# A decoder trunk on one core: work ordered by tasks in hand-written code, or by a list scheduler over a recorded graph

## The chip, the cores and the metric

The kernel runs on one core of a Trainium2 chip. The core's engines work side by side, each through its own list of instructions in the order in which the list was written: TensorE (PE) multiplies matrices, VectorE (DVE) and ScalarE (ACT) do elementwise work, GpSimd (POOL) helps them, and SyncE (SP) issues transfers between HBM and the on-chip memory. The metric is the device time of one launch in microseconds (us), lower is better.

## The reference

Two layers of a hybrid decoder; 256 prompt tokens and 8 sample tokens (264 columns in all) share the weights. In outline:

```python
def token_mixers(u, lp, ...):
    proj = u @ lp['w_in']                       # 2048 -> 5504 with padding
    (q, k, v, z, xbc, dt, mq, mk, mv, mo, mi, mf) = split(proj)
    att = swa_prompt(q, k, v, sinks) / swa_sample(...)      # window 128, cached keys for the samples
    y   = ssd_scan(causal_conv(xbc), dt, A, B, C, S0)       # Mamba-2, chunks of 128
    y   = rms_norm((y + d_skip * xs) * silu(z), ssm_norm)   # two groups of 512
    h   = rms_norm(mlstm_scan(mq, mk, mv, mi, mf, C0, n0, m0)) * sigmoid(mo)
    return concatenate([att, y, h]) @ lp['w_out'], new_states
def decoder_layer(x, lp, ...):
    x = x + token_mixers(rms_norm(x, norm_mix), lp, ...)
    u = rms_norm(x, norm_mlp)
    return x + square(relu(u @ lp['w_up'])) @ lp['w_down']
```

A final RMSNorm follows. The new key, value, convolution, SSM and mLSTM states are outputs too.

## The kernel before

Weights stream from HBM once. The unit is a **half**: a block of 8 x 128 x 128 weights, 512 KB, 748 of them. SP loads it (`raw`), ACT casts it to a rounded form (`hi`, L163), DVE subtracts to get the remainder (`lo`, L164), and PE multiplies it in 24 matmuls of 264 columns: 16 with `hi` against the two parts of the activations (L1249, L1250), 8 with `lo` (L1252). `raw`, `hi` and `lo` have three buffers each, so the splits can be at most three halves ahead. Two halves make a **group** of 128 output columns of `w_in`.

In each layer the halves come in this order: `w_in` 86 halves (groups: gates, k, v, q, convolution B/C, convolution x, then 12 groups m of the mLSTM, 8 groups z that gate the SSD's output, 4 groups o), `w_out` 32 halves (the first 16 need the mix tiles `hA`/`lA`, the other 16 `hB`/`lB`), then the MLP's 256. The halves of layer 0 are numbered 0 to 373, those of layer 1 from 374.

The mixers' own small work (attention, SSD scan, mLSTM, norms) is woven between the halves. It is written as Python generators, "tasks", in the list `active`. Before each half the main loop lets the tasks go on until their stated costs pass `BUDGET = 1.7`, with flags (`setf`, `wait`) that keep a step back by one or more halves:

```python
        run_evacs()
        load(i + 4)
        cut(i + 2)
        run_later()
        run_tasks()
```

So the order on every engine is that of the source's own steps. Small PSUM results take four `ms` and two `sg` buffers, sums of halves two `acc`. The norm of the SSD's output, `y_norm`, is run once for each of two groups of 512: a matmul with ones spreads the sum of squares (`ms<-ysq`, L198), eight DVE steps take the inverse root (`rsqrt`, L168 to L175), then `xs` is scaled (L1042), cast and split into `hA`/`lA` or `hB`/`lB`.

Of the kernel before, what the change touches and what calls it, by code (L numbers as in the profile page):

```python
# [17 lines left out]
L = 2  # L18
P = 128
# [21 lines left out]
def trunk(ctx, tc, I, O):  # L41
    nc = tc.nc
    vec, act, pool, pe = nc.vector, nc.scalar, nc.gpsimd, nc.tensor
# [38 lines left out]
    slot = [0]  # L82
    flags = {}
    active = []
    evacs = []
    later_ = []

    def setf(name):
        flags[name] = slot[0]

    def ok(name, lag=1):
        return name in flags and slot[0] >= flags[name] + lag

    def wait(*names, lag=1):
        while not all(ok(n, lag) for n in names):
            yield 0.0

    def later(fn, n=1):
        later_.append((slot[0] + n, fn))

    def run_later(force=False):
        due = [x for x in later_ if force or x[0] <= slot[0]]
        for x in due:
            later_.remove(x)
            x[1]()

    def run_tasks():
        spent = 0.0
        for g in list(active):
            try:  # L110
                spent += next(g)
            except StopIteration:
                active.remove(g)
            if spent > BUDGET:
                break

    def run_evacs():
        while evacs:
            fn, need = evacs[0]
            if not all(ok(n) for n in need):  # L120
                return
            evacs.pop(0)
            fn()

    def tick():
# [7 lines left out]
    xt = cp.tile([P, KB, T], F32, name="xt")  # L133
    cst = cp.tile([P, C_SEL], F32, name="cst")
    cst2 = tb([P, C_N - C_SEL])
    vecs = [cp.tile([P, V_N], F32, name=f"vec{l}") for l in range(L)]
    wfin = cp.tile([P, KB], F32, name="wfin")
# [3 lines left out]
    ones = cp.tile([P, P], F32, name="ones")  # L141
    zeros = cp.tile([64, P], F32, name="zeros")
    sgn = cp.tile([P, 1], F32, name="sgn")
    pool.memset(ones, 1.0)
    warm = st((P, 1), "coef")
    A(out=warm, in_=ones[:, 0:1], func=AF.Exp)
    pool.memset(zeros, 0.0)
    pool.memset(sgn, 1.0)
    pool.memset(sgn[32:64], -1.0)
    identb = cp.tile([P, P], BF16, name="identb")  # L150
    maskb = cp.tile([P, 2, P], BF16, name="maskb")
    sel = cp.tile([P, 64], F32R, name="sel")
    ssel = cp.tile([P, 24], F32R, name="ssel")

    uh = cp.tile([P, KB, T], F32R, name="uh")
    ul = cp.tile([P, KB, T], F32R, name="ul")
    ssq = cp.tile([P, T], F32, name="ssq")
    rb = cp.tile([P, T], F32, name="rb")
    UU = [(uh[:, k], ul[:, k]) for k in range(KB)]

# [5 lines left out]
    def rsqrt(y, v, t):  # L166
        """y = v ** -0.5: a first guess from the bits, then a step of third order and one of second order."""
# [1218 lines left out]
```

## Time and profile before

| | |
|---|---|
| three runs | 2396.3, 2398.72, 2400.55 us; median 2398.72 |
| profiled execution, its span (first to last instruction) | 2391.9 us |
| profiled execution, around its span | not given apart; 2398.72 - 2391.9 = 6.8 us if it ran at the median |
| PE busy | 2327.1 us, 97% of the span |
| DVE busy | 1509.1 us, 63% |
| ACT busy | 1097.3 us, 46% |
| POOL busy | 435.9 us, 18% |
| mean granted TensorE clock | 0.993 |

The span covers the work between the first and the last instruction. Busy time is a sum over the whole span and says nothing of a single stretch: the mixers of layer 0 lie at about 40 to 452 us, its MLP up to 1199 us, the mixers of layer 1 at 1199 to 1629 us, its MLP up to 2376 us, and the final norm behind.

### The profile page before, as it was taken

Reading aid. Unit: us, or ns where it says so; the run is one execution under the profiler, and the core shown is the slowest. Engines: PE = TensorE matmul, PEld = TensorE weight load, DVE = VectorE, ACT = ScalarE, POOL = GpSimd, SP = SyncE. Lnnn points to the kernel's source line nnn. Section 1 sums busy time; section 2 is a strip of 40 time slices with the busy share of each in tenths; the row PEclk is TensorE's granted clock in tenths of the full one; section 3 lists DMA queues with packets and bytes.
Section 4 is the critical chain, followed back from the end, with each engine's and each line's share of the span. In section 5 each row is a group of like instructions: output and inputs, shape, how many; then the busy total and the mean of one; then the engine's idle time right before and its main releaser. Section 6 shows DMA issues by size and latency. Waiting matters only on the chain.

```text
span 2391.9 us, 45993 instructions
## 1 busy us (share of the span) xinstructions
PE 2327.1 (97%) x18874; PEld 2305.8 (96%) x18874; DVE 1509.1 (63%) x2179; ACT 1097.3 (46%) x1700; POOL 435.9 (18%) x408
## 2 busy tenths in 40 slices
PE   7999989999999999999999999999999999999997
PEld 7898989999999999999999989899999999999997
DVE  8778996754555454455686799866545545544544
ACT  5545544543353354354445454445434434534542
POOL 4226541400000000001441274332000000000023
PEclk9999999999999999999999999999999999999998
DMA  7456766555555555555554566555555555555553
GB/s 238 141 165 197 197 202 187 177 183 180 183 179 184 178 184 178 184 181 181 179 177 136 177 213 187 177 179 182 180 183 179 182 181 184 178 183 179 184 178 132
DMA packets 123474, 432.26 MB, mean 181 GB/s; under 512 B 15744, under 2 KB 18432, under 8 KB 123264
## 3 DMA queue, kind: packets, MB, share of 16 engines
q1 hardware_dynamic: 122688, 428.10, 56.9%
q8 instruction: 149, 2.44, 0.4%
q10 hardware_dynamic: 576, 1.22, 0.1%
q14 instruction: 61, 0.50, 0.1%
HBM read 410.10 MB, written 19.16 MB: 179 GB/s over the span
## 4 chain that ended last, share of the span: by engine, by line
PE 88%; DVE 9%; issue 1%; ACT 1%; POOL 1%; DMA 0%; DVEq 0%; ACTq 0%; POOLq 0%
PE acc L1250 28%; PE acc L1252 28%; PE acc L1249 28%; DVE lo L164 3%; DVE eB L669 1%; PE ms L685 0%; DMA raw<-in_w_in 0%; PE ms L468 0%; PE sg L447 0%; DVE ra L1027 0%; DVE tb L971 0%; PE ms L460 0%; DVE xt L1262 0%; ACT uh L179 0%; DVE ul L182 0%
## 5 line engine op out<-in xcount | busy, mean ns | idle before, releaser
L163 ACT CAST hi<-raw 128x1024 fp32r<-128x1024 f32 x748 | 786.3, 1051 | 1046.5 <-PE acc L1250 969.6
L164 DVE TENSOR_TENSOR lo<-raw,hi 128x1024 fp32r<-128x1024 f32 x745 | 931.7, 1251 | 347.0 <-ACT hi L163 346.4
L1249 PE MATMUL acc<-uh,hi 128*128 128x264 f32 x3392 | 859.1, 288 | 6.8 <-ACT uh L179 6.8
L1250 PE MATMUL acc<-ul,hi 128*128 128x264 f32 x3392 | 854.0, 287 | 4.3 <-DVE ul L182 4.3
L1249 PEld LDWEIGHTS acc<-uh,hi 128*128 128x128 f32 x3392 | 643.7, 190 | 10.1 <-ACT uh L179 6.8
L1250 PEld LDWEIGHTS acc<-ul,hi 128*128 128x128 f32 x3392 | 645.3, 190 | 8.2 <-DVE ul L182 5.0
L1252 PE MATMUL acc<-uh,lo 128*128 128x264 f32 x3392 | 481.0, 283 | 3.4 <-DVE lo L164 3.4
L1252 PEld LDWEIGHTS acc<-uh,lo 128*128 128x128 f32 x3392 | 442.9, 189 | 3.8 <-DVE lo L164 3.8
L1249 PE MATMUL acc<-hA,hi 128*128 128x264 f32 x1280 | 316.2, 283 | 0.0
L1249 PE MATMUL acc<-hB,hi 128*128 128x264 f32 x1280 | 316.2, 283 | 0.0
L1250 PE MATMUL acc<-lB,hi 128*128 128x264 f32 x1280 | 315.4, 283 | 0.0
L1250 PE MATMUL acc<-lA,hi 128*128 128x264 f32 x1280 | 315.4, 283 | 0.0
L187 POOL TENSOR_TENSOR ssq<-xt 128x264 f32<-128x264 f32 x4 | 6.1, 1522 | 1431.4 <-DVE xt L1143 1313.7
L1249 PEld LDWEIGHTS acc<-hB,hi 128*128 128x128 f32 x1280 | 241.3, 189 | 0.0
L1249 PEld LDWEIGHTS acc<-hA,hi 128*128 128x128 f32 x1280 | 241.3, 189 | 0.0
L1250 PEld LDWEIGHTS acc<-lB,hi 128*128 128x128 f32 x1280 | 240.3, 188 | 0.0
L1250 PEld LDWEIGHTS acc<-lA,hi 128*128 128x128 f32 x1280 | 240.3, 188 | 0.0
L1143 DVE TENSOR_TENSOR xt<-acc,xt 128x264 f32<-128x264 f32 x128 | 55.3, 432 | 205.0 <-PE acc L1252 205.0
L1252 PE MATMUL acc<-hB,lo 128*128 128x264 f32 x1280 | 183.2, 285 | 0.0
L1252 PE MATMUL acc<-hA,lo 128*128 128x264 f32 x1280 | 183.2, 285 | 0.0
L1135 DVE SCALAR_TENSOR_TENSOR ra<-acc,rb 128x264 f32<-128x264 f32 x128 | 55.3, 432 | 196.8 <-PE acc L1252 196.7
L1252 PEld LDWEIGHTS acc<-hB,lo 128*128 128x128 f32 x1280 | 167.0, 188 | 0.0
(394 smaller groups left out, 1861.0 us busy)
## 6 DMA issues: line engine op xcount, KB each, us to landing
raw<-in_w_up SPq DMA_DIRECT2D x256, 512.0 KB, 3.6
raw<-in_w_down SPq DMA_DIRECT2D x256, 512.0 KB, 3.6
raw<-in_w_in SPq DMA_DIRECT2D x172, 512.0 KB, 3.7
raw<-in_w_out SPq DMA_DIRECT2D x64, 512.0 KB, 3.6
S<-in_ssm SPq DMA_DIRECT2D x16, 512.0 KB, 4.6
out_ssm_s<-S SPq DMA_DIRECT2D x16, 512.0 KB, 2.8
S<-in_mC SPq DMA_DIRECT2D x8, 512.0 KB, 4.6
out_C_s<-S SPq DMA_DIRECT2D x8, 512.0 KB, 3.1
```

The costliest lines, as they stand in the source:

```text
L163: act.copy(out=hi, in_=src)
L164: (f or tt)(out=lo, in0=src, in1=hi.bitcast(F32), op=SUB)
L187: f(out=total, in0=src, in1=src, op=MUL)
L669: tt(out=wT[:, i], in0=E[:, i], in1=cbg, op=MUL)
L1135: stt(out=r, in0=acc, scalar=0.0, in1=rb, op0=MAX, op1=MUL)
L1143: tt(out=xt[:, g], in0=acc, in1=xt[:, g], op=ADD)
L1249: pe.matmul(acc, lhsT=h[:, k], rhs=rh, start=it.first and k == 0, stop=False)
L1250: pe.matmul(acc, lhsT=h[:, k], rhs=rl, start=False, stop=False)
L1252: pe.matmul(acc, lhsT=o[:, k], rhs=it.rhs(k)[0], start=False, stop=it.last and k == 7)
```

## The change

The code that computes is kept, but instructions are no longer issued when the source reaches them. `Program.record` writes each down as a node of a graph, with the regions of tiles that it reads and writes; `price` gives it a cost from a formula; `issue` first works backwards through the graph for a time by which each node is due, and then forwards through a model of five engines: it picks, again and again, the instruction that can start first. `emit` hands a free buffer to each tile at that moment (three `raw`/`hi`/`lo`, four `ms`, two `sg`, two `acc`, as before). Tasks, flags, `wait`, `BUDGET` and `tick` go away. The diff, cut to its core:

```diff
-BUDGET = 1.7
...
-    for i, it in enumerate(items):
-        slot[0] += 1
...
-        run_evacs()
-        load(i + 4)
-        cut(i + 2)
-        run_later()
-        run_tasks()
...
+class Program:
+    LAG = 0.06
+    AHEAD = 6.0
+    EARLY = 30.0
+    LOOSE = ("ms", "sg", "ra", "ac", "eA", "eB")
...
+        def room(n):
...
+                if not empty or (q[h] is not s and (len(empty) < 2 or s.tag not in self.LOOSE)):
+                    return None
...
+                for n in seen:
+                    a = room(n)
+                    if a is None:
+                        continue
+                    r = max(n.ready, a)
+                    s = max(t, r)
+                    k = (max(s - t, 0.08), self.rank(e, n))
+                    if pick is None or k < pick[0]:
+                        pick = (k, s, n)
...
+            if n.port:
+                n.cost += 0.6 * min(n.cost, max(0.0, port["POOL" if e == "DVE" else "DVE"] - s))
...
+    def rank(self, e, n):
+        if e == "PE":
+            return (n.weight, n.i)
+        return (min(n.kind, 1), n.due)
...
+        for ks in (range(0, 4), range(4, 8)):
+            with pr.bundle(True):
...
+        if l == 0:
+            accs = [acc_tile(), acc_tile(), ms_tile([P, T]), ms_tile([P, T])]
+            for g, acc in enumerate(accs):
+                half(acc, I["w_in"][l, g][:, 0:8], u_rhs(0), True, False)
```

Two things follow from these lines. On PE `rank` puts any small matmul that is ready ahead of a bundle of weight matmuls. And `room` gives a buffer of a tag to the tile that is next in the program's order, or, for the tags in `LOOSE`, to another one only while two buffers are empty. The last lines let the first four groups of layer 0 do their first halves before their second ones, with four accumulators. The splits of the attention's part of the mix move into `y_norm`. The counts of instructions are the same on each engine; what changes is their order and which buffer each uses. Every instruction of the kernel after carries the line of `emit`, L398.

PE, layer 0, the first `y_norm`. Before, its spreading matmul stands between the halves 71 and 72 (`acc_3443` and `acc_3583` are sums of `w_in`):

```order
L1252 MATMUL acc_3443<-uh_86,lo_3362 128x264 x8
L198 MATMUL ms_3551<-ysq_3186,ones_73 128x264
L970 MATMUL ms_3575<-srow_3237,ssel_85 128x512
L970 MATMUL ms_3579<-srow_3237,ssel_85 128x512
L1249 MATMUL acc_3583<-uh_86,hi_3413 128x264
```

In the changed kernel it stands behind the last half of `w_in` (85) and just ahead of half 86, the first of `w_out`, which needs its result in `hA_2619` and `lA_2703` (`acc_4176` is the sum of half 86, `acc_4212` that of half 87):

```order
L398 MATMUL ms_4133<-ysq_3305,ones_69 128x264
L398 MATMUL sg_4451<-srow_3578,ssel_220 128x512
L398 MATMUL sg_4804<-srow_3578,ssel_220 128x512
L398 MATMUL sg_4503<-srow_3578,ssel_220 128x512
L398 MATMUL acc_4176<-hA_2619,hi_3977 128x264
L398 MATMUL acc_4212<-hA_2619,hi_4023 128x264
L398 MATMUL ms_4170<-ysq_4148,ones_69 128x264
L398 MATMUL acc_4176<-lA_2703,hi_3977 128x264
L398 MATMUL acc_4176<-hA_2619,hi_3977 128x264
L398 MATMUL acc_4212<-lA_2703,hi_4023 128x264
L398 MATMUL acc_4176<-lA_2703,hi_3977 128x264
L398 MATMUL acc_4176<-hA_2619,hi_3977 128x264
```

The norm moved 14 halves later, and no half of `w_in` is left between it and the one that reads its result.

DVE, the same norm. Before, its steps are spread out between the splits of four halves (`lo<-raw,hi`):

```order
L164 TENSOR_TENSOR lo<-raw,hi 128x1024
L202 TENSOR_SCALAR ysq<-ms 128x264
L971 TENSOR_TENSOR tb<-ms,S_3439 128x512 x2
L1027 SCALAR_TENSOR_TENSOR ra<-ac,ra 128x264
L168 TENSOR_SCALAR Bb<-ysq 128x264
L1028 TENSOR_TENSOR xs<-xs,ra 128x264
L164 TENSOR_TENSOR lo<-raw,hi 128x1024
L169 SCALAR_TENSOR_TENSOR ac<-Bb 128x264
L975 TENSOR_REDUCE cqs<-tb 128x4
L170 TENSOR_TENSOR ac<-ac,ysq 128x264
L171 SCALAR_TENSOR_TENSOR ac<-ac 128x264
```

In the changed kernel the steps follow on rows of the mLSTM's sample work (`mw`, `sb`, `cqs`, `ns`, `tb<-sg,S`); the first row is the split of half 88:

```order
L398 TENSOR_TENSOR lo<-raw,hi 128x1024
L398 COPY mw<-ms 128x2
L398 SCALAR_TENSOR_TENSOR lB<-lB,EG,ms 128x129 x4
L398 TENSOR_TENSOR tb<-sg,S_4050 128x512
L398 COPY mw<-ms 128x2
L398 COPY sb<-ms 128x64
L398 SCALAR_TENSOR_TENSOR mw<-mw 128x4
L398 TENSOR_REDUCE cqs<-tb 128x4
L398 TENSOR_TENSOR ns<-m_1826,sb 128x32
L398 TENSOR_SCALAR ysq<-ms 128x264
L398 TENSOR_TENSOR mw<-mw,q2c 128x4
L398 SCALAR_TENSOR_TENSOR ms_4173<-sb 128x32
```

Behind these come 35 more rows without a split; the next `lo`, of half 89, is the 47th row behind that of half 88. What was spread over several halves now stands in one block.

SP, the very start. Before, one block of weights goes first, then `vecs` and most of the input `xt<-in_x`:

```order
L1182 DMA raw<-in_w_in 128x1024
L1196 DMA vec_70<-in_vecs 128x131
L1193 DMA xt<-in_x 128x528 x2
L1193 DMA xt<-in_x 128x1056 x2
L1182 DMA raw<-in_w_in 128x1024
L1193 DMA xt<-in_x 128x1056
L1182 DMA raw<-in_w_in 128x1024
L1204 DMA tb<-in_cst 128x344
```

Now three blocks of weights go ahead of all of `x`:

```order
L398 DMA raw<-in_w_in 128x1024 x3
L398 DMA vec_80<-in_vecs 128x131
L398 DMA xt<-in_x 128x528 x2
L398 DMA xt<-in_x 128x1056 x3
L398 DMA cst<-in_cst 128x656
L398 DMA scv<-in_scv 128x384
L398 DMA tb<-in_cst 128x344
L398 DMA S_105<-in_kt 128x1032
L398 DMA S_107<-in_vc 128x1024
```

The first `x` thus stands behind two more blocks of 512 KB in the queue.

## Rows read from the trace of the kernel before

**Rows 1.** The page: busy time, chain that ended last, the splits' group.

```profile
PE 2327.1 (97%) x18874; PEld 2305.8 (96%) x18874; DVE 1509.1 (63%) x2179; ACT 1097.3 (46%) x1700; POOL 435.9 (18%) x408
...
PE 88%; DVE 9%; issue 1%; ACT 1%; POOL 1%; DMA 0%; DVEq 0%; ACTq 0%; POOLq 0%
...
L164 DVE TENSOR_TENSOR lo<-raw,hi 128x1024 fp32r<-128x1024 f32 x745 | 931.7, 1251 | 347.0 <-ACT hi L163 346.4
```

**Rows 2.** Windows: the span by stages; busy us of each engine, its instructions in brackets.

```profile
core 0: us, PE busy (x) PEld busy (x) DVE busy (x) ACT busy (x) POOL busy (x), PEclk, DMA share, GB/s
0.00:40.00 40.00, 27.23 (x188) 25.77 (x189) 30.19 (x45) 23.24 (x37) 17.42 (x26) 1.00 0.72 248
40.00:166.00 126.00, 120.47 (x979) 118.29 (x978) 99.79 (x211) 64.86 (x124) 36.26 (x71) 1.00 0.50 158
166.00:196.00 30.00, 29.24 (x214) 26.38 (x213) 20.34 (x24) 12.16 (x23) 9.11 (x5) 1.00 0.58 178
196.00:270.00 74.00, 68.89 (x544) 67.17 (x544) 69.52 (x90) 38.05 (x114) 55.38 (x23) 0.98 0.64 215
270.00:359.00 89.00, 80.11 (x612) 77.60 (x611) 80.47 (x159) 43.03 (x112) 35.99 (x30) 0.96 0.69 192
359.00:452.00 93.00, 93.00 (x768) 93.00 (x768) 67.58 (x101) 45.62 (x57) 33.71 (x29) 1.00 0.60 184
452.00:1199.00 747.00, 746.88 (x6151) 746.61 (x6150) 395.52 (x475) 331.45 (x401) 36.11 (x32) 1.00 0.58 181
...
1250.00:1343.00 93.00, 91.69 (x747) 90.14 (x747) 68.57 (x142) 50.84 (x101) 19.18 (x46) 1.00 0.48 151
1343.00:1373.00 30.00, 29.30 (x215) 26.44 (x213) 20.26 (x23) 12.31 (x24) 9.12 (x5) 1.00 0.56 174
1373.00:1447.00 74.00, 68.78 (x540) 67.07 (x541) 69.25 (x90) 37.25 (x114) 55.29 (x23) 0.98 0.65 215
1447.00:1536.00 89.00, 80.44 (x614) 77.93 (x613) 80.65 (x159) 43.94 (x113) 34.57 (x26) 0.96 0.59 177
...
2376.00:2392.00 16.00, 0.72 (x3) 0.30 (x2) 10.62 (x23) 0.51 (x1) 3.59 (x4) 0.60 0.35 135
```

**Rows 3.** Waits of PE: matmul and releaser: us in total, times, longest.

```profile
PE ms L685 <- DVE eB L669: 11.8, 10, 1.8
PE ms L981 <- DVE tb L971: 10.1, 4, 3.2
...
PE acc L1252 <- DVE lo L164: 3.4, 2, 2.7
```

**Rows 4.** Timeline of DVE in layer 0's SSD: start us, us, instruction.

```profile
225.05 3.08 DVE L164 TENSOR_TENSOR lo<-raw,hi 128x1024 fp32r<-128x1024 f32 x1
...
230.22 1.21 DVE L164 TENSOR_TENSOR lo<-raw,hi 128x1024 fp32r<-128x1024 f32 x1
...
238.69 0.94 DVE L669 TENSOR_TENSOR eB<-eA,lA 128x256 f32<-128x256 f32 x2 [1.14 <-ACT eA L665]
```

**Rows 5.** Timeline of POOL, same stretch.

```profile
224.66 2.39 POOL L777 TENSOR_TENSOR S<-S,tb 128x1024 f32<-128x1024 f32 x1
```

**Rows 6.** DVE groups by shape, 0 to 470 us: busy us, mean ns.

```profile
L164 DVE TENSOR_TENSOR lo<-raw,hi 128x1024 fp32r<-128x1024 f32 x123 | 161.3, 1312 | 17.3 <-ACT hi L163 17.1
...
L669 DVE TENSOR_TENSOR eB<-eA,lA 128x256 f32<-128x256 f32 x16 | 18.4, 1169 | 2.4 <-ACT eA L665 2.1
```

**Rows 7.** Timeline of DVE in the second `y_norm` of layer 0.

```profile
353.41 0.43 DVE L202 TENSOR_SCALAR ysq<-ms 128x264 f32<-128x264 f32 x1
353.75 0.18 DVE L1001 SCALAR_TENSOR_TENSOR ms<-ms,ms 128x32 f32<-128x32 f32 x1
...
354.20 0.43 DVE L169 SCALAR_TENSOR_TENSOR ac<-Bb 128x264 f32<-128x264 f32 x1
```

**Rows 8.** Timeline of PE, two of its first matmuls.

```profile
9.56 0.42 PE L1250 MATMUL acc<-ul,hi 128*128 128x264 f32 x1
9.78 0.42 PE L1249 MATMUL acc<-uh,hi 128*128 128x264 f32 x1
```

More of the change, by code (lines that the diff above doesn't have):

```diff
@@ L79, in tb @@
         return st(shape, "tb", bufs=2)
[L82 to L125, printed above, removed]
-        slot[0] += 1
-        run_evacs()
-        run_later()
-        run_tasks()
[L133 to L137, printed above, removed]
+    xt = st((P, KB, T), "xt")
+    cst = st((P, C_SEL), "cst")
+    cst2 = tb((P, C_N - C_SEL))
+    vecs = [st((P, V_N), f"vec{l}") for l in range(L)]
+    wfin = st((P, KB), "wfin")
     ident = cst[:, C_ID:C_ID + P]
@@ L140, in trunk @@
     sinT = cst[:, C_SIN:C_SIN + T]
[L141 to L159, printed above, removed]
+    ones = st((P, P), "ones")
+    zeros = st((64, P), "zeros")
+    sgn = st((P, 1), "sgn")
+    identb = st((P, P), "identb", BF16)
+    maskb = st((P, 2, P), "maskb", BF16)
+    sel = st((P, 64), "sel", F32R)
+    ssel = st((P, 24), "ssel", F32R)
+    uh = st((P, KB, T), "uh", F32R)
+    ul = st((P, KB, T), "ul", F32R)
+    ssq = st((P, T), "ssq")
+    rb = st((P, T), "rb")
     def split(hi, lo, src, f=None):
@@ L346, in gates_rows @@
             xp = ms_tile([P, 8, 16])
-            for j in range(8):
-                pe.matmul(xp[:, j], lhsT=psel[:, j], rhs=Rb[:, 0:16], start=True, stop=True)
+            with pr.bundle():
+                for j in range(8):
+                    pe.matmul(xp[:, j], lhsT=psel[:, j], rhs=Rb[:, 0:16], start=True, stop=True)
             act.copy(out=EX, in_=xp)
-            yield 0.3
             xp = ms_tile([P, 16])
@@ L649, in final_state @@
                 tt(out=so, in0=s1, in1=so, op=ADD)
[L650 removed]
+                sync.dma_start(out=O["ssm_p"][l, :, fs], in_=so)
             ybank = {}
@@ L855, in mlstm @@
             tt(out=n0s, in0=n0s, in1=kws, op=ADD)
-            later(lambda: nc.sync.dma_start(out=O["n_s"][l], in_=n0s))
+            sync.dma_start(out=O["n_s"][l], in_=n0s)
             for h0 in (0, 2):
                 cp_ = ms_tile([P, 2, 130])
-                for h in range(2):
-                    pe.matmul(cp_[:, h, 0:129], lhsT=kw[:, 0, h0 + h], rhs=vt1[:, 0, h0 + h, 0:129], start=True, stop=True)
+                with pr.bundle():
+                    for h in range(2):
+                        pe.matmul(cp_[:, h, 0:129], lhsT=kw[:, 0, h0 + h], rhs=vt1[:, 0, h0 + h, 0:129], start=True, stop=True)
@@ new lines, in mlstm @@
+                sw = eB([P, 4, P])
+                tt(out=sw, in0=qkp, in1=E, op=MUL)
+                nps = []
+                for h0 in (0, 2):
+                    np_ = ms_tile([P, 2, 130])
+                    with pr.bundle():
+                        for h in range(2):
+                            hh = h0 + h
+                            pe.matmul(np_[:, h, 0:129], lhsT=sw[:, hh], rhs=vt1[:, c, hh, 0:129], start=True, stop=c == 0)
+                            if c == 1:
+                                pe.matmul(np_[:, h, 0:129], lhsT=qg[:, hh], rhs=C0[:, hh, 0:129], start=False, stop=True)
+                    nps.append(np_)
@@ L1208, in trunk @@
-    cut(0)
+    pool.memset(ones, 1.0)
+    warm = st((P, 1), "coef")
+    A(out=warm, in_=ones[:, 0:1], func=AF.Exp)
+    pool.memset(zeros, 0.0)
+    pool.memset(sgn, 1.0)
+    pool.memset(sgn[32:64], -1.0)
+    sync.dma_start(out=vecs[0], in_=I["vecs"][0])
+    for a, b in ((0, 2), (2, 4), (4, 8), (8, 12), (12, 16)):
+        sync.dma_start(out=xt[:, a:b], in_=I["x"][:, a:b])
+    sync.dma_start(out=cst2, in_=I["cst"][:, C_SEL:C_N])
+    sync.dma_start(out=cst, in_=I["cst"][:, 0:C_SEL])
+    sync.dma_start(out=wfin, in_=I["wfin"])
```

1127 lines of the change are left out of this document (617 added, 510 removed).

## The prediction

> **What bounds the kernel now.** I began with the page: PE is busy 97% of the span and carries 88% of the chain that ended last, DVE 9% [rows 1]. So the kernel is a stream of weight matmuls, and only the places where PE is kept from its full pace can give time back. The table by stages shows these places. Its yardstick is the stretch 359 to 452 us, in which PE never pauses: 93 us for 768 matmuls, 0.1211 us each [rows 2]; a half of 24 takes 2.91 us. A stage's length less its matmul count times 0.1211 us is what it loses. The reader should see how unevenly this lies [rows 2]. Layer 0's mixers lose 126 - 979 x 0.1211 = 7.4, then 4.1, 74 - 544 x 0.1211 = 8.1 and 89 - 612 x 0.1211 = 14.9 us, together 34.5. The four stages of layer 1 lose 2.5, 4.0, 8.6 and 14.6, together 29.7. The MLP loses 747 - 6151 x 0.1211 = 2.1 us, the start 40 - 188 x 0.1211 = 17.2, the tail nearly its whole 16. (Small matmuls are some longer and some shorter than 0.1211; summed by kind they even out.) About 64 us in the two mixers are thus what another order could reach at all.
>
> What stands behind these losses is told by the waits and by DVE's share. PE's largest waits are for DVE: `eB` 11.8 us in 10 times, `tb` 10.1 us in 4, `lo` 3.4 in 2 [rows 3]. In the two worst stages DVE is busy 69.5 of 74 and 80.5 of 89 us; in the one behind it is busy 67.6 of 93, in the MLP 395.5 of 747 [rows 2]. DVE is full in the middle of the mixers and has room on both sides.
>
> **The change part by part.** Counts of instructions on each engine are the same, so nothing is added or removed; only order and buffers move. I costed the new order thus: between two neighbouring halves I summed PE's and DVE's instructions, each by the mean duration of its kind in the trace of before, and let the splits be three halves (9 us) ahead at most, as the three `lo` buffers allow. Where DVE's sum outruns PE's by more than that lead, PE waits. These sums are estimates.
>
> Start: now three blocks of weights go ahead of `x`, so its first matmul comes later, but four groups do their first halves before any second half and so use each arriving part of `x` four times. Matmuls done by 30 us come out at some 114 in place of 109: 0 us, with 3 either way.
>
> Layer 0. The gates' chain makes DVE's sum 46 us against PE's 37 in the halves 8 to 20: less the 6 us of lead there, about 4 us lost. The attention and the SSD move together: PE's small matmuls, ready ones first, stand in halves 40 to 47 (52 us of PE, 35.5 of DVE); round trips from PE through ACT and DVE between them, some 3 us. DVE follows with a crowd: 43 us in halves 46 to 50, where PE has about 20 behind a lead of 16; the splits of 49 and 50 come some 7 us late. The mLSTM's stretch then has DVE near PE's pace: 1 us. Last, the SSD's norm now stands directly ahead of half 86, and its 8 DVE steps stand among mLSTM rows in a block of 46 rows without a split. A wide step with a narrow one behind takes 354.20 - 353.75 = 0.45 us [rows 7]. Eight such pairs are 3.6 us, the rows ahead of and between them 5 (the means of their kinds), the first `xs`, its cast and its remainder 2; after the split of half 88 (1.2 us [rows 4]) that is some 12 us until PE may run freely, of which 3 to 5 are covered by PE's small matmuls and the pieces of halves 86 and 87 that can go. I take 9, with 5 (all cover counts) and 14 (POOL in the way) as bounds. In the kernel before this norm was hidden by 14 halves of `w_in`, 41 us. Sum for layer 0: 4 + 3 + 7 + 1 + 9 = 24 in place of 34.5, a gain of 10.5.
>
> Layer 1 gets another order: its norm stands two to six halves earlier, with halves of `w_in` behind it, so there is no such block. What I find is 5 us at the gates, 2 in the attention's round trips, 5 in a crowd of DVE of 30 us against PE's 16 less a lead of 9, 3 to 4 near its norm. That is 15 to 16 in place of 29.7, a gain of 14.5. `w_out`, the MLPs and the tail keep their order and cost nothing more: there DVE has slack of 67.6 of 93 us and less [rows 2]; layer 0's first 16 `w_out` halves do take 24 us more of DVE, within 47 us of PE.
>
> Sum: 0 - 10.5 - 14.5 = -25 us. The profiled span of 2391.9 us would be 2367. The median of the runs, 2398.7, stands 6.8 us above that span, and I let it stay so: 2398.7 - 25 = 2373.7, rounded to 2373.
>
> **A price that speaks against it.** A `lo` that began 0.4 us after a long POOL operation took 3.08 us in place of 1.21 [rows 4], and it ended 1.08 us after POOL did (225.05 + 3.08 against 224.66 + 2.39 [rows 5]): it stood still until POOL was through. The change's cost model books for such a meeting 0.6 x the operation's cost at most, 0.6 x 1.2 = 0.72 us, where 1.87 were lost. Whatever it plans around these meetings comes 1.15 us late each.
> The Trainium skill states this as a rule (page "SBUF — State Buffer", section on the two separate sides): the port pair that DVE and GpSimd share is an exclusive lock, and whichever comes second fully blocks until the first is done. By that rule, the row agrees: 1.87 us, not 0.72.
>
> **The rivals.** *Full recovery.* The scheduler knows every dependence, and DVE's total over 40 to 452 us is 99.8 + 20.3 + 69.5 + 80.5 + 67.6 = 338 of 412 us [rows 2], so PE could be fed all the way; then some 45 of the 64 us come back: 2354. Against it stands the order itself around half 86.
> *Nothing gained.* In 196 to 359 us DVE is busy 150 of 163; if its crowd only moves from there to halves 46 to 50 and 86 to 101, PE waits as long in other places: 2394 to 2400.
> *Slower, by collisions of DVE with POOL.* In the first 470 us `lo` averages 1.312 us against 1.21, 123 x 0.10 = 12 us, and the 16 `eB` 1.169 against an undisturbed 0.94 / 2 = 0.47, 11 us [rows 4, 6]: some 23 us in a layer that are lost to meetings already. POOL's updates of the state, 8 in a layer's SSD and as long as the 2.39 us one [rows 5], are not the only ones. If the crowded DVE stretches meet POOL twice as often, and PE waits there, that is 2 x 23 = 46 us more: 2373 + 46 = 2419. It decides from 25 / 1.87, about 14 further meetings in places where PE has no lead left.
> A smaller cost goes with each pause of PE: its first matmuls stand 0.22 us apart [rows 8], not 0.12, and in the two worst stages the granted clock is 0.98 and 0.96 [rows 2]; a pause of 9 us at half 86 may add 2 us.
>
> **How the numbers follow.** The forecast (2360 to 2384, a gain of 15 to 39) gets 0.50. Full recovery (below 2360) 0.18. A gain too small for the sum, 5 to 15 us, 0.12; nothing gained, within 0.2% or 4.8 us, about what a measurement of this kernel can tell from no change, 0.07; slower 0.13. Faster is 0.50 + 0.18 + 0.12 = 0.80. The range leaves out about 0.07 below and 0.13 above: 2348 to 2396, which holds both bounds of the norm's block and of the start.
>
> **What the profile after would show.** If right: matmul counts by stage as before, the losses in layer 0's mixers near 24 us and in layer 1's near 15; one wait of PE of 5 to 14 us for `hA` or `lA` at the first half of `w_out` of layer 0 and none such in layer 1; waits for `lo` grown from 3.4 us to some 10, waits for `eB` and `tb` shrunk; DVE's busy time within 20 us of 1509. The first 40 us should hold 188 matmuls, give or take 25. Wrong would be: DVE's busy time up by 30 us or more with `lo` and `eB` means above 1.31 and 1.17 (collisions); waits spread over all halves (the planned times don't hold on the chip); or no wait at half 86 and losses near 10 us in a layer.

## The result: 1.3% slower, and the profile after

The changed kernel takes 2426.68 us (median of 4 runs, 2425.59 to 2432.91) against 2398.44 us before: a ratio of 1.0126, 95% interval 1.0112 to 1.0140. The forecast was 2373 us, range 2348 to 2396; the time lies above it, on the side that had a chance of 0.13. The profiled execution's span is 2425.3 us, 33.4 more than before, at a mean granted clock of 0.985 (0.993 before).

The page of the changed kernel: busy time, the chain that ended last, the splits' group (before: [rows 1]).

```profile
PE 2341.6 (97%) x18874; PEld 2320.0 (96%) x18874; DVE 1515.9 (63%) x2179; ACT 1098.1 (45%) x1700; POOL 434.0 (18%) x408
...
PE 83%; DVE 7%; issue 4%; POOL 3%; DMA 2%; ACT 1%; SPq 0%; DVEq 0%; POOLq 0%; ACTq 0%
...
L398 DVE TENSOR_TENSOR lo<-raw,hi 128x1024 fp32r<-128x1024 f32 x745 | 949.7, 1275 | 363.9 <-ACT hi L398 359.8
```

No engine has more instructions: DVE's busy time is up by 7 us, PE's by 14.5, the rest is nearly unchanged. That PE waits more shows on this page only in the chain, where its share falls from 88% to 83%. So the view to read is the table by stages, with the yardstick of the prediction, 0.1211 us a matmul (before: [rows 2]):

```profile
0.00:40.00 40.00, 27.22 (x193) 26.22 (x194) 28.08 (x41) 23.82 (x36) 15.22 (x27) 1.00 0.77 265
40.00:166.00 126.00, 118.65 (x935) 117.15 (x934) 100.54 (x205) 61.39 (x108) 40.60 (x76) 0.96 0.52 162
166.00:240.00 74.00, 70.34 (x526) 65.95 (x526) 54.71 (x79) 37.33 (x107) 27.73 (x14) 0.95 0.40 130
240.00:270.00 30.00, 26.94 (x213) 25.99 (x213) 28.39 (x29) 11.80 (x35) 27.17 (x10) 1.00 0.71 242
270.00:359.00 89.00, 83.35 (x652) 80.85 (x651) 72.04 (x114) 43.64 (x104) 32.98 (x25) 0.98 0.63 205
359.00:452.00 93.00, 83.32 (x663) 82.03 (x662) 74.21 (x145) 42.33 (x69) 32.02 (x29) 0.94 0.58 177
...
1199.00:1250.00 51.00, 50.76 (x414) 50.21 (x412) 41.30 (x74) 20.91 (x25) 17.52 (x20) 1.00 0.58 179
1250.00:1343.00 93.00, 86.84 (x665) 85.57 (x666) 61.20 (x138) 48.20 (x108) 21.41 (x45) 0.94 0.41 126
1343.00:1373.00 30.00, 30.00 (x237) 28.47 (x236) 24.98 (x53) 16.70 (x33) 5.16 (x11) 1.00 0.41 134
1373.00:1447.00 74.00, 61.52 (x459) 57.92 (x458) 64.29 (x69) 30.46 (x84) 51.43 (x24) 0.94 0.62 197
1447.00:1536.00 89.00, 82.97 (x638) 81.56 (x639) 72.57 (x107) 38.91 (x95) 38.89 (x23) 0.95 0.71 196
1536.00:1629.00 93.00, 92.52 (x754) 91.86 (x753) 78.19 (x149) 45.61 (x80) 18.76 (x17) 1.00 0.58 181
1629.00:1660.00 31.00, 31.00 (x257) 31.00 (x256) 24.99 (x32) 16.45 (x22) 24.71 (x22) 1.00 0.56 180
```

From 40 to 452 us PE did 935 + 526 + 213 + 652 + 663 = 2989 matmuls; 412 - 2989 x 0.1211 = 50.0 us are lost there, 34.5 before. Stage by stage the losses are 12.8, 10.3, 4.2, 10.0 and 12.7. In layer 1 some 45 us are lost (its mixers take 446.1 us instead of 430.6, and 29.7 + 15.5 = 45). These 15.5 us in each layer are 31 of the 33.4; the rest is spread over the MLPs. The two layers lose them differently. In layer 0 the loss ahead of 359 us is hardly larger than before (37.3 us against 34.5), and the last stage, which lost nothing before, adds 12.7. In layer 1 the last two rows lose next to nothing and the middle rows lose more.

Two things make up the 15.5. PE's idle time in 40 to 452 us is 412 - 382.6 = 29.4 us, where before it was 412 - 391.7 = 20.3: 9 us. The other 6 are matmuls that took longer: the clock column stands at 0.94 to 0.98 in four of these five stages, before at 0.98 and 0.96 in two and at 1.00 in the rest [rows 2]. In the clock's own records PE stands at the lower of its two levels (1.2 GHz) for 58 us of the two mixers, before for 20.5. Layer 1 divides in the same way: idle 461 - 435.6 = 25.4 us in 1199 to 1660, before 16.3 in 1199 to 1629, 9 us again.

PE's waits (matmul and releaser: us in total, times, longest; before: [rows 3]). The largest, 10.3 us for `uh` at the start, is left out; it is no part of the mixers.

```profile
PE ms L398 <- DVE m L398: 10.0, 2, 5.8
PE sg L398 <- DVE tb L398: 8.5, 7, 3.0
PE sg L398 <- DVE prod L398: 8.2, 3, 4.1
PE ms L398 <- ACT lA L398: 4.6, 1, 4.6
PE acc L398 <- DVE lo L398: 4.2, 4, 2.3
PE acc L398 <- ACT hA L398: 4.0, 1, 4.0
PE acc L398 <- DVE m L398: 3.6, 4, 1.0
PE ms L398 <- POOL Qm L398: 3.5, 2, 2.2
PE ms L398 <- POOL ysq L398: 3.2, 2, 2.7
```

Before, two patterns that came again and again (`eB`, `tb`) held most of the waiting. `eB` is nearly gone, 1.9 us, as forecast; `tb` has shrunk only from 10.1 us to 8.5, and `lo` has grown to 4.2 us, not to the 10 that were expected. In place of the pattern stand single waits, each for another step of a chain, and 38 of the 50 us shown are waits of a small matmul (`ms`, `sg`).

The timeline of PE at half 86 (start, us, instruction, idle before and its releaser):

```profile
362.79 0.49 PE L398 MATMUL sg<-srow,ssel 128*128 128x512 f32 x1 [2.98 <-DVE tb L398]
367.30 0.81 PE L398 MATMUL acc<-hA,hi 128*128 128x264 f32 x2 [4.02 <-ACT hA L398]
370.79 1.25 PE L398 MATMUL ms<-ysq,ones 128*128 128x264 f32 x2 [2.68 <-POOL ysq L398]
```

This is the norm's block that the prediction named: 2.98 + 4.02 + 2.68 = 9.7 us idle against the 9 it took. Counted by matmuls from the start, the changed kernel was 17 matmuls or 2.1 us behind at 359 us, and 123 matmuls or 14.9 us behind at 376.

### The profile page after: what moved, and what is told of

Its sections match the earlier page's. It is cut to its first block, busy times and chain, and to the rows that moved or that the text cites. A ratio compares the mean times of both kernels' runs of the same rounds, so it can differ in the third digit from the quotient of the medians.

```text
span 2425.3 us, 46071 instructions
## 1 busy us (share of the span) xinstructions
PE 2341.6 (97%) x18874; PEld 2320.0 (96%) x18874; DVE 1515.9 (63%) x2179; ACT 1098.1 (45%) x1700; POOL 434.0 (18%) x408
## 4 chain that ended last, share of the span: by engine, by line
PE 83%; DVE 7%; issue 4%; POOL 3%; DMA 2%; ACT 1%; SPq 0%; DVEq 0%; POOLq 0%; ACTq 0%
PE acc L398 80%; PE ms L398 3%; DVE lo L398 2%; PE sg L398 1%; DMA raw<-in_w_in 1%; DVE m L398 1%; DVE tb L398 1%; POOL S L398 1%; ACT hi L398 1%; POOL tb L398 0%; DMA S<-in_ssm 0%; DVE mw L398 0%; DVE ac L398 0%; POOL ysq L398 0%; DVE lA L398 0%
## 5 line engine op out<-in xcount | busy, mean ns | idle before, releaser
L398 ACT CAST hi<-raw 128x1024 fp32r<-128x1024 f32 x748 | 785.2, 1050 | 1033.7 <-PE acc L398 943.9
L398 DVE TENSOR_TENSOR lo<-raw,hi 128x1024 fp32r<-128x1024 f32 x745 | 949.7, 1275 | 363.9 <-ACT hi L398 359.8
L398 PE MATMUL acc<-uh,hi 128*128 128x264 f32 x3392 | 860.9, 288 | 13.9 <-ACT uh L398 10.3
L398 PE MATMUL acc<-ul,hi 128*128 128x264 f32 x3392 | 854.6, 286 | 2.5 <-DVE ul L398 2.5
L398 PEld LDWEIGHTS acc<-uh,hi 128*128 128x128 f32 x3392 | 643.7, 190 | 15.7 <-ACT uh L398 10.3
L398 PEld LDWEIGHTS acc<-ul,hi 128*128 128x128 f32 x3392 | 645.8, 190 | 5.2 <-DVE ul L398 3.1
L398 PE MATMUL acc<-uh,lo 128*128 128x264 f32 x3392 | 485.6, 286 | 4.5 <-DVE lo L398 4.2
L398 PEld LDWEIGHTS acc<-uh,lo 128*128 128x128 f32 x3392 | 442.9, 189 | 6.4 <-DVE lo L398 5.8
L398 PE MATMUL acc<-hA,hi 128*128 128x264 f32 x1280 | 319.2, 285 | 4.0 <-ACT hA L398 4.0
L398 PE MATMUL acc<-lA,hi 128*128 128x264 f32 x1280 | 319.0, 285 | 0.0
L398 PE MATMUL acc<-hB,hi 128*128 128x264 f32 x1280 | 317.8, 284 | 0.0
L398 PE MATMUL acc<-lB,hi 128*128 128x264 f32 x1280 | 317.6, 284 | 0.0
L398 POOL TENSOR_TENSOR ssq<-xt 128x264 f32<-128x264 f32 x4 | 6.2, 1539 | 1381.4 <-DVE xt L398 1381.4
L398 PEld LDWEIGHTS acc<-hA,hi 128*128 128x128 f32 x1280 | 241.8, 189 | 4.6 <-ACT hA L398 4.3
L398 PEld LDWEIGHTS acc<-lA,hi 128*128 128x128 f32 x1280 | 241.2, 189 | 0.3
L398 PEld LDWEIGHTS acc<-lB,hi 128*128 128x128 f32 x1280 | 241.0, 188 | 0.0
L398 PEld LDWEIGHTS acc<-hB,hi 128*128 128x128 f32 x1280 | 240.8, 188 | 0.0
L398 DVE TENSOR_TENSOR xt<-acc,xt 128x264 f32<-128x264 f32 x192 | 82.9, 432 | 241.9 <-PE acc L398 241.8
L398 PE MATMUL acc<-hA,lo 128*128 128x264 f32 x1280 | 181.0, 283 | 0.0
L398 PE MATMUL acc<-hB,lo 128*128 128x264 f32 x1280 | 180.5, 283 | 0.0
L398 DVE SCALAR_TENSOR_TENSOR ra<-acc,rb 128x264 f32<-128x264 f32 x128 | 55.4, 433 | 197.7 <-PE acc L398 197.6
L398 PEld LDWEIGHTS acc<-hA,lo 128*128 128x128 f32 x1280 | 165.6, 188 | 0.0
```

Of the source, the lines that this page charges most:

```text
L398: getattr(eng, method)(*[real(a) for a in args], **{k: real(a) for k, a in kw.items()})
```

## The experiments

The theory from these rows: half 86 is the cause, since the norm waits for an `ms` buffer, and the clock and the meetings of DVE with POOL add to it. (A meeting is a DVE and a POOL operation that want to run at the same time, where the second stands still.) Rivals: the meetings alone; the planned distance of PE's small matmuls, that is the time that the plan leaves between a matmul and the step that it reads; the price that the plan puts on DVE. Each ratio is to the kernel before in runs beside it, whose medians lie at 2394.9 to 2395.8 us.

**e1, the norm may take any empty `ms` buffer.**

```diff
-  if not empty or (q[h] is not s and (len(empty) < 2 or s.tag not in self.LOOSE)):
+  if not empty or (q[h] is not s and s.name != "yn" and (len(empty) < 2 or s.tag not in self.LOOSE)):
```

> One edit to the changed kernel: the PSUM tile of y_norm's spreading matmul may take any empty ms buffer; all else is planned by the same rules. Theory A (the order in which ms buffers are handed out put the norm directly ahead of half 86): the first ms<-ysq runs many halves earlier, the waits of PE for hA and ysq there (4.0 and 2.7 us, with the clock at half) vanish, 2426.7 - 11 = 2416 us. Rival (the mLSTM's late chain is the true cause and the norm only its first victim): a stall as long comes back before half 102, 2424 to 2430 us.

Measured: 2445.83 us, ratio 1.0210 (1.0195 to 1.0225). Windows of e1 at the old place and at two later ones:

```profile
359.00:376.00 17.00, 17.00 (x140) 16.88 (x139) 13.53 (x17) 6.42 (x13) 4.51 (x3) 1.00 0.75 246
400.00:412.00 12.00, 5.29 (x30) 5.11 (x30) 4.42 (x8) 1.05 (x1) 0.00 (x0) 0.72 0.61 71
424.00:436.00 12.00, 7.24 (x31) 6.79 (x32) 8.07 (x26) 4.49 (x8) 1.97 (x2) 0.51 0.34 131
```

PE is busy all through half 86, and loses 12 - 30 x 0.1211 = 8.4 and 12 - 31 x 0.1211 = 8.2 us at half 102 (a wait of 6.7 us for `xt`) and behind it. The pause was removed and the time not, so half 86 alone is not the cause. The edit also gave all later work another order; whether the same delay fell due later or a new one was made is not shown.

**e2, small matmuls planned 2.0 us later than what they read.**

```diff
+                 + (self.MARGIN if m.eng == "PE" and e != "PE" and not m.weight else 0.0)
```

> One edit: the planner takes a small matmul on PE to be ready 2.0 us after its operands' planned end, so it stands later in PE's order, behind weights that are ready. Theory B (small matmuls stand just in time by a plan that is too early, and PE waits in its order): PE's waits for operands of small matmuls, 18.5 us in layer 0 and 23.9 in layer 1, fall below 10 each, 2400 to 2408 us. Rival C (it is the runs of small matmuls that cost, by the clock and by starving DVE): waits shrink a little, the time with the clock at half in the mixers stays near 58 us, 2418 to 2430 us.

Measured: 2424.92 us, 1.0126 (1.0111 to 1.0141), as after. Layer 1's idle time (pauses over 0.15 us) fell from 25.2 to 19.1 us, layer 0's rose from 28.9 to 32.7.

**e3 and e4, a limit on small matmuls in a row** (0.2 and 0.5 us), so that weight matmuls stand between them.

```diff
-  k = (max(s - t, 0.08), self.rank(e, n))
+  k = (max(s - t, 0.08), (n.weight != (run > self.RUN), n.i) if e == "PE" else self.rank(e, n))
```

> One edit: after more than 0.2 us of small matmuls in a row the planner takes a bundle of weights next on PE if one is ready, so small matmuls stand between the weights as in the kernel before. Theory C (runs of small matmuls lower the clock and let DVE run dry, then crowd it): time with the clock at half in the mixers falls from 58 us to 20 to 30, PE's busy time from 2341.6 to about 2328, 2396 to 2406 us. Rival B (planned just in time): PE's waits for small operands stay above 35 us, 2418 us or more.

> The edit of e3_runs_02 with 0.5 us in place of 0.2. Theory C: between the changed kernel and e3_runs_02, nearer the latter, 2400 to 2412 us, and clock at half 25 to 40 us in the mixers. Rival B: no order between the two, both near 2420 us.

Measured: e3 2424.43 us, 1.0124 (1.0107 to 1.0141); e4 2422.94, 1.0115 (1.0100 to 1.0130). A few us at most. PE's time at the lower clock in layer 1's mixers went from 27.3 to 17.1 us in e4.

**e5 and e6, both kernels without POOL's long state updates.** In their place stand memsets of the same tiles, which read nothing; the new sample states of SSM and mLSTM are left out.

```diff
+  if n.eng == "POOL" and method == "tensor_tensor" and kw["out"].store.tag in ("S0", "tb"):
+      eng.memset(real(kw["out"]), 0.0)
+      continue
```

(This is e5's; e6 writes `pool.memset` at the five places of the kernel before.)

> The changed kernel in the same order, but the long POOL updates of the sample states (S<-S, tb<-Bb,dtx: 28 to 30 in a layer) are issued as memsets of the same tiles, which read nothing; the new sample states are left out of the computation. Theory D (DVE stands still behind these updates just where PE waits for it next): DVE's busy time falls by 50 us or more of 1515.9, the waits of PE for m, prod, eB and lo shrink, 2380 to 2395 us, and the distance to e6_before_quiet_pool is under 10 us in place of 28 to 31. Rival E (the order itself is at fault, whatever POOL does): distance to e6 stays above 20 us.

> The kernel before with the same POOL updates issued as memsets, the new sample states left out. Its waits for eB (11.8 us) and some of those for tb go by both theories: 2375 to 2388 us. Theory D: within 10 us of e5. Rival E: 20 us or more faster than e5.

Measured: e5 2388.42 us, 0.9972 (0.9960 to 0.9984); e6 2356.47 us, 0.9838 (0.9823 to 0.9852). So the updates cost 37 to 38 us in the kernel after and 39 in the kernel before (2395.6 beside it), about the same, and the two orders stay 32 us apart without them. More meetings are not why the change is slower. Two reservations. With the updates more goes than the meetings: in the kernel after ACT stood 30.1 us for POOL to be done with a buffer (`Bb`, read by `tb<-Bb,dtx`), before 0.2, in e5 not at all.

```profile
ACT Bb L398 <- POOL tb L398: 30.1, 7, 5.6
```

And the cost depends on the order: by the same edit e13 gets 51.5 us faster (e15), e9 25.9 us (e12). PE's waits in e6 over the whole span, the three largest:

```profile
PE acc L1248 <- ACT uh L179: 6.8, 1, 6.8
PE acc L1249 <- DVE ul L182: 4.7, 3, 2.1
PE acc L1251 <- DVE lo L164: 3.3, 1, 3.3
```

The first two are the start. Without the updates the hand-made order has hardly a wait for small steps.

In layer 0 the place of the difference shows. From 40 to 320 us e5 did 2180 matmuls and e6 2190, 1.2 us apart; from 320 to 359 us 209 and 317, 13.1 us apart. That is the norm's block again, idle for 2.62 + 3.33 + 2.68 = 8.6 us with POOL's long updates gone. Its window in e5:

```profile
340.00:357.00 17.00, 9.53 (x44) 8.51 (x45) 14.16 (x39) 3.97 (x13) 6.46 (x8) 0.60 0.38 83
```

In layer 0, without the updates, the planned order is thus as good as the hand-made one up to the norm. Layer 1, where e5 is 12.7 us longer than e6 (426.0 against 413.3), has no such block.

**e7 and e8, a stricter price of the meetings.** In e7 an instruction with two operands in SBUF is planned only after the other engine's has ended. The edit, cut here to its core, also prices POOL's two-operand instructions lower and counts no memset and no one-operand instruction as a meeting; e8 joins it to e1.

```diff
+  if n.port:
+      s = max(s, port["POOL" if e == "DVE" else "DVE"])
...
-      n.cost += 0.6 * min(n.cost, max(0.0, port["POOL" if e == "DVE" else "DVE"] - s))
```

> The changed kernel with the planner's model of DVE and POOL as the traces show them: an operation with two operands in SBUF cannot start before the other engine's running one ends (in place of a surcharge of 0.6 x its cost), and a long POOL update costs 2.2 us. Theory D: the plan then holds on the chip, PE's idle time in the mixers falls from 54 us to under 36, the time with the clock at half from 58 us to under 30, 2395 to 2408 us. Rival E: idle time stays, 2415 us or more.

> e7_lock_aware and the edit of e1_norm_any_slot together. Theory D with theory A: the second norm of each layer comes earlier too, 3 to 8 us faster than e7_lock_aware. Rival: as in e1, a later stall takes its place, no faster than e7 by more than 2 us, or slower.

Measured: e7 2445.92 us, 1.0210 (1.0193 to 1.0227); e8 2451.26, 1.0236 (1.0221 to 1.0251). Worse than after, but not in the mixers: from 40 us on, e7's two layers of mixers take as long together as those of the kernel after (872.8 us against 872.7), and its 19 us stand in the two MLPs, 757 to 758 us each against 748. Near their starts PE waits once for 5 us, behind a norm's steps on DVE, and the clock falls:

```profile
487.25 0.56 PE L398 MATMUL acc<-uh,hi 128*128 128x264 f32 x1 [5.06 <-DVE ra L398]
```

So the stricter price gained nothing where the meetings are, and lost where there are hardly any.

**e9 and e12, the edits of e2 and e4 together**, in e12 without POOL's updates as in e5.

> The edits of e2 and e4 together: small matmuls planned 2.0 us behind their operands, and at most about 0.5 us of them in a row. Theory F (PE's order lacks what the kernel before had in both ways, a half of distance between operand and matmul and a limit on what is done in one go; each alone only moves the waits): idle time of PE in the mixers under 40 us (54 in the changed kernel), clock at half under 30 us (58), 2400 to 2412 us. Rival G (the waits come from the order on DVE, which neither edit touches): 2418 us or more.

> e9 with the POOL updates of e5 issued as memsets (new sample states left out). Theory F: the order is then as good as that of before, so within 10 us of e6 (2356.5), 2350 to 2366. Rival G: waits of PE for DVE stay even without collisions, 2375 us or more.

Measured: e9 2435.74 us, 1.0172 (1.0156 to 1.0188); e12 2409.88, 1.0059 (1.0040 to 1.0077). In e12 layer 1's mixers took 419.3 us (e5 426.0, e6 413.3) with 8.7 us idle, layer 0's 441.4 from 30 us on (e5 416.1, e6 402.4) with 28.8: better in one layer, much worse in the other. Distance and limit together thus made the kernel slower than either alone with the updates (2435.7 against 2424.9 and 2422.9), and slower than e5 by 21 us without them.

**e10 and e11, the kernel before with other budgets**, to see whether its order is a lucky one: `BUDGET` 5.0 in place of 1.7, and flags with no lag.

```diff
-BUDGET = 1.7
+BUDGET = 5.0
...
-        return name in flags and slot[0] >= flags[name] + lag
+        return name in flags
```

> The kernel before with BUDGET 5.0 in place of 1.7: its tasks run in larger lumps between two halves, nothing else changes. Theory F: lumps alone make it slower, by runs of small matmuls and by splits that come late: 2403 to 2425 us, more time with the clock at half than 20.5 us. Rival G: its distance of a half is kept, so it stays within 5 us of 2396.

> The kernel before in which a step may be issued in the same half as the one that it depends on (the flags' distance of one or two halves is taken out; BUDGET stays 1.7). Theory F: small matmuls stand just behind the instructions that make their operands, PE's waits for them grow past 60 us, 2405 to 2430 us. Rival G: within 5 us of 2396, since DVE's load per half is unchanged.

Measured: e10 2397.89 us, 1.0010 (1.0000 to 1.0020); e11 2403.74, 1.0034 (1.0021 to 1.0047). Neither edit upsets the order by hand; without its lags, which are a distance too, it loses 8 us, short of the theory's 2405 and beyond the rival's 5.

**e13, DVE priced at its pitch.** Instructions of DVE that follow each other directly start 0.08 us before the profile's end of the one ahead (the median in the trace of after); the plan books the whole duration and 0.03 us more.

```diff
-  return 0.155 + n / (1920 if fast else 960), 0.0, fast or len(sbuf) > 1, 0
+  return 0.07 + n / (1920 if fast else 960), 0.085, fast or len(sbuf) > 1, 0
...
-  free[e] = s + n.cost + (0.0 if e == "PE" else 0.03)
+  free[e] = s + n.cost + (0.0 if e in ("PE", "DVE") else 0.03)
```

> Only the price of a DVE instruction in the scheduler changes: its pitch as the trace of after shows it (back-to-back instructions overlap by 0.08 us, and no 0.03 us gap). Theory (DVE is taken for full, so the norm's chain is put off): the wait at half 86 goes, DVE's backlog there too, and some 10 to 20 us come back: 2405 to 2417 us, PE's idle time in layer 0's mixers from 28.9 to 20 us or less. Rival (the price does not matter, the order fails where DVE meets POOL and in the chains of small steps): 2420 to 2445 us, the idle time still 25 us or more in each layer, only elsewhere.

Measured: 2444.45 us, 1.0204 (1.0189 to 1.0219). Half 86 begins at 373.4 us and half 102 at 420.0, 46.6 us for 16 halves: no pause there. But it begins 6 us later than after, and layer 1's idle time is 36.6 us. Its largest wait in the mixers:

```profile
PE ms L398 <- DVE m L398: 24.5, 5, 8.1
```

The theory that DVE's price makes the loss falls. As in e1, the pause at half 86 went and as much or more was lost elsewhere.

**e14 and e16, e13 with the rule of e7 and with the limit of e4.**

> As e13, and the scheduler lets a DVE or POOL instruction that reads two operands from SBUF begin only when the other engine's has ended. Theory (DVE's price had left the planner no room to move around the meetings; with room it does): faster than e13 by 5 to 15 us, 2395 to 2410. Rival (the planned meetings do not fall where the chip has them): no better than e13, 2415 to 2450, as the same rule alone made it worse (2445.9).

> As e13, and at most 0.5 us of small matmuls in a row on PE, so that weight matmuls stand between them. Theory (two separate losses, the backlog of DVE and the clock's falls in runs of small matmuls, add up): 4 to 10 us faster than e13, time at half the clock in the mixers under 40 us. Rival (the runs are an effect of the waits and go with them): within 3 us of e13.

Measured: e14 2422.23 us, 1.0116 (1.0099 to 1.0133); e16 2437.55, 1.0175 (1.0160 to 1.0190). The stricter price now gains 22 us where it lost 19 alone (e7), so the two prices do depend on each other; but 2422 is only the time of after. The limit gains 7 us on e13 (e16), within its theory's 4 to 10.

**e15 and e18, the order of e13 without the meetings, then with e2's distance as well.** The new sample states are left out as in e5.

> The order of e13, with POOL's long updates of the sample states as memsets (the new sample states of SSM and mLSTM are left out), as in e5 and e6. Without the meetings the kernel before took 2356.5 and after 2388.4. Theory (the price of DVE makes the difference of 32 us): 2356 to 2368. Rival (something else in the order does): 2380 to 2395.

> The order of e15 with one edit more: a small matmul may be planned only 2.0 us after the end of what it reads from another engine (e2's edit). The new sample states are left out as in e15. Theory (PE stands without distance behind chains of small steps): idle time in the mixers from 16.1 and 12.0 us to under 9 each, 2365 to 2380 us. Rival (the distance only moves the waits to weight matmuls and DVE, as in e2): 2385 to 2410.

Measured: e15 2392.99 us, 0.9994 (0.9984 to 1.0004), the rival's value. PE's largest waits in e15 behind the start's:

```profile
PE ms L401 <- DVE m L401: 6.6, 3, 3.9
PE sg L401 <- DVE prod L401: 5.2, 2, 3.1
PE ms L401 <- POOL ysq L401: 4.7, 2, 3.1
```

Single small steps again, with the long updates gone; the `m` waits were 24.5 us in e13, so most of those went with the updates. e18: 2374.15 us, 0.9913 (0.9897 to 0.9928), 18.8 us less than e15 by the distance alone. The first two rows there:

```profile
PE ms L403 <- DVE m L403: 5.0, 3, 2.7
PE sg L403 <- DVE prod L403: 3.8, 2, 3.2
```

Idle time fell from 16.1 and 12.0 us to 13.6 and 5.8, PE's time at the lower clock from 17.1 and 6.8 to 6.8 and 0. The idle time is 8.7 us of the gain; the clock is worth at most some 8 more, an estimate from 0.22 us a matmul at the lower level [rows 8] against 0.12. Layer 1's mixers take 413.7 us, with the hand-made order 413.3 (e6): level. Layer 0's still take 9 us more (411.6 against 402.4). The theory's 9 us idle was missed in layer 0; its time, 2365 to 2380, came.

**e17, the kernel before with the SSM's sample states taken off POOL.** All is computed.

```diff
-  ptt(out=s0, in0=s0, in1=EX[:, :, b].unsqueeze(2).to_broadcast([P, 8, P]), op=MUL)
+  for j in range(8):
+      A(out=s0[:, j], in_=s0[:, j], func=AF.Copy, scale=EX[:, j, b:b + 1])
...
-  ptt(out=s0, in0=s0, in1=tbt, op=ADD)
+  for j in range(8):
+      stt(out=s0[:, j], in0=Bb[:, j // 4], scalar=dtx[:, j, b:b + 1], in1=s0[:, j], op0=MUL, op1=ADD)
```

> The kernel before, with the 8 updates of the SSM's sample states in a layer taken off POOL: the product with EX as 8 ACT activations of 128x128 each, the product with dtx and the sum as 8 DVE instructions of 128x128 (scalar, multiply, add) each. All is computed. POOL loses 60 us in a layer, ACT gains some 19 us, DVE 8 x 8 x 0.2 = 13 us. Theory (meetings of DVE and POOL cost 38 us, most of them with these three long operations): DVE's time lost in meetings falls from 36 to 10 to 15 us in a layer, and the kernel gets faster, 2365 to 2380 us. Rival (the added 13 us of DVE in its fullest stretch and ACT's blocks of 2.4 us cost as much as the meetings): 2390 to 2400.

Measured: 2380.78 us against 2395.61 beside it, 0.9938 (0.9925 to 0.9950): faster than the kernel before by 0.6%, just outside its theory's 2365 to 2380. Its groups from 30 to 480 us, which hold layer 0's mixers:

```profile
L770 ACT ACTIVATE S<-S,EX 128x128 f32<-128x128 f32 x64 | 19.6, 389 | 2.0 <-DVE tb L768 2.0
...
L164 DVE TENSOR_TENSOR lo<-raw,hi 128x1024 fp32r<-128x1024 f32 x128 | 159.6, 1247 | 22.1 <-ACT hi L163 21.8
L776 DVE SCALAR_TENSOR_TENSOR S<-Bb,dtx,S 128x128 f32<-128x128 f32 x64 | 18.2, 348 | 0.2 <-ACT S L770 0.2
```

The new DVE instructions took 0.35 us each, not 0.2, so they cost 18 us in a layer in place of 13; the kernel before has the same instruction and shape in `xs<-xs,vec,ms`, at 0.337 us. DVE's time beyond its undisturbed durations (an estimate, with the median of each shape in e5 and e6 as undisturbed) fell from 36 to 14 us in each layer, and `lo` from 1.312 us [rows 6] to 1.247.

## Why the prediction was wrong, by its steps

**Start.** Right: 193 matmuls in the first 40 us, 188 before, so 16.6 us lost against 17.2.

**The norm's block at half 86.** Right in place and size, though as three waits and not the single one for `hA` or `lA` that was expected: 9.7 us idle against 9, and with the clock at 0.70 in 359 to 376 us a loss of 17 - 37 x 0.1211 = 12.5 against 9 + 2:

```profile
359.00:376.00 17.00, 7.32 (x37) 6.03 (x36) 15.55 (x46) 4.14 (x16) 8.68 (x10) 0.70 0.30 92
```

**The rest of layer 0: the step that failed.** It was forecast at 4 + 3 + 7 + 1 = 15 us in place of 34.5 and is 50.0 - 12.7 = 37.3: nothing came back, and the norm's block came on top. The step is the way in which PE's waits were costed. The sums of PE's and DVE's work between two halves, with three halves of lead, let PE wait only where DVE's sum outruns PE's, and 3 us were added for round trips through other engines. The actual waits stand where there was work enough for all: 40 to 166 us lost 12.8 where 4 were booked, with waits of 1.98 (`ra`), 4.06 (`prod`) and 1.30 us (`Qm`), each for one small step of a chain that passes from engine to engine. PE takes its list in order, so the weight matmuls behind a small one wait as well: during the wait for `prod`, which ended at 71.95 us, a split had been done by 68.62, and the next weight matmul came at 77.51, behind the small ones.

**Layer 1: the same step.** 15 to 16 us were forecast, some 45 measured. The norm itself stood well there, as expected, with no block. Three waits make 14.6 of some 25 us idle:

```profile
1409.96 1.11 PE L398 MATMUL ms<-cst,lA 128*128 128x128 f32 x4 [4.64 <-ACT lA L398]
1447.98 0.48 PE L398 MATMUL ms<-cst,m 128*128 128x128 f32 x1 [5.83 <-DVE m L398]
1482.80 0.33 PE L398 MATMUL ms<-cst,m 128*128 128x128 f32 x1 [4.12 <-DVE m L398]
```

Each is for a small step, but what stood ahead of the step differs. Ahead of the first, ACT had waited 4.72 us for POOL's `tb` before it could go on to the next casts. Ahead of the second, DVE stood behind POOL with two `lo` (the rows under the price of the meetings). Ahead of the third, DVE and ACT had nothing to do for 7.44 and 6.57 us, since a block of weights was late: issued at 1467.13 us behind the state output `out_C_p`, which landed at 1478.68, it landed at 1479.99, in 12.9 us where the median is 3.8.

```profile
1480.09 1.04 ACT L398 CAST hi<-raw 128x1024 fp32r<-128x1024 f32 x1 [6.57 <-DMA raw<-in_w_in]
```

The sums by engine hold none of these: they take every instruction at its mean, and every operand as there when its turn comes.

**Is it the short planned distance?** The order of PE's list sets a small matmul right where the plan has its operand ready, so whatever comes late holds PE up. The planned times were not printed beside the measured ones; that steps come late against the plan is inferred from the waits. For distance as the remedy speaks e18 against e15, 18.8 us, with layer 1 level with the hand-made order. Against it as the whole cause speak the other runs with it: e2 against after, 2 us, with POOL's full work; e9 against e4, 13 us slower; e12, with the limit too, 21 us slower than e5; and e11, in which the kernel before loses only 8 us without its lags. Edits to the plan moved the time by up to some 20 us, mostly for the worse and without a pattern that was forecast, so one pair of orders does not settle it. What is shown is that the waits for single steps and the lower clock hold the lost time; why this order has so many of them is shown in part only.

**The clock.** 2 us were added for one pause. PE's idle time explains 9 of 15.5 us in a layer; the other 6 are lost while PE is busy, 13 in the two layers. This term was mis-sized: there are many pauses in place of one, and a fall without a pause (below).

**The price of the meetings.** The lock itself is as the prediction had it. DVE and POOL after, in layer 1:

```profile
1439.81 5.92 DVE L398 TENSOR_TENSOR lo<-raw,hi 128x1024 fp32r<-128x1024 f32 x2
...
1438.54 3.26 POOL L398 TENSOR_TENSOR S<-S,tb 128x1024 f32<-128x1024 f32 x1
1441.95 2.70 POOL L398 TENSOR_TENSOR tb<-Bb,dtx 128x1024 f32<-128x1024 f32 x1
```

Two `lo` took 5.92 us, 2.42 undisturbed, and the second ended 1439.81 + 5.92 - 1441.95 - 2.70 = 1.08 us after POOL's second operation, the same 1.08 as in [rows 4, 5]. The Trainium skill (page "SBUF — State Buffer", section on the two separate sides) calls it an exclusive lock in which the second comer waits to the end; these rows agree. But the rival "slower, by collisions" is refuted although its 2419 us came near, by luck: DVE's time beyond undisturbed durations (estimated as for e17) was 36 us in each layer before and 37 to 38 after, not twice as much. They moved from `eB` (1.169 to 0.548 us in layer 0) to `lo` (1.312 to 1.387), and e5 and e6 price the updates alike.

**"Full recovery"** failed with the forecast's step: knowing every dependence, and having DVE's total fit, did not keep PE fed. The prediction's sign of failure, "waits spread over all halves (the planned times don't hold on the chip)", comes nearest to what the profile shows; it was given no chance and no price of its own.

**What stays open.** With POOL's full work neither the distance (e2, 2424.9) nor DVE's price (e13, 2444.5) helped. Two runs are missing: e18's two edits with full work, and the distance alone without the updates. So how the 28 us divide between short distance, meetings and steps that come late for other reasons is not settled. Nor is layer 0's remaining 9 us in e18.

## What to carry to other kernels

Where every engine takes its list in order, it is not enough that the sums of work fit. For the engine that is the bound, look at each small instruction, at what it reads, and at what stands ahead of that step on its own engine: here three waits of small matmuls went back to a buffer, a meeting and a late block of weights. Removing the largest pause tells nothing until the span falls: in e1 and e13 the pause at half 86 went and the time did not. Where a new plan reorders everything, compare more than one pair of plans before an edit gets the credit: the same distance gave back 18.8 us in one order, 2 in another and cost 13 in a third. Where two engines share a lock, taking the long operation off one of them (e17, -0.6%) paid where planning around it (e7) gained nothing in the mixers.

## What the hardware showed unexpectedly

The granted clock fell to 0.50, the lower level of 1.2 GHz, while PE was busy by the profile all the time. Windows of the kernel after in layer 1 (the third number from the right is the granted clock):

```profile
1316.00:1322.00 6.00, 6.00 (x50) 5.82 (x49) 2.16 (x7) 2.88 (x8) 0.00 (x0) 1.00 0.28 91
1323.00:1329.00 6.00, 6.00 (x30) 6.00 (x30) 1.00 (x4) 1.68 (x6) 0.00 (x0) 0.50 0.19 76
```

PE's timeline there:

```profile
1320.77 0.93 PE L398 MATMUL ms<-pT,S 128*128 128x8 f32 x7
1321.55 0.41 PE L398 MATMUL ms<-adg,ones 128*128 128x64 f32 x2
1321.80 2.85 PE L398 MATMUL ms<-tb,eB 128*128 128x64 f32 x16
```

What PE did just before the fall, at 1322.6 us, was a run of matmuls of 8 and 64 columns, without a gap. The 30 matmuls in 1323 to 1329 us took 0.20 us each on average, the 50 in 1316 to 1322 us 0.12, but their shapes differ, so this is not the price of the clock alone. The limits on such runs (e3, e4) lowered the time at the lower clock in part and the kernel's time by 2 to 4 us, so why it fell there is not shown.
